# Two lists for the work on the cached keys and the norms, and other steps for each

## The chip, the cores and the metric

The kernel runs on one core of one Trainium2 chip. The metric is the device time of one execution in microseconds. The kernel before was run three times: 2337.23, 2340.57 and 2343.8 us, median 2340.57 us.

## What is computed

One layer of a streaming encoder. A prompt of 2048 rows and a sample of 8 x 16 rows (8 running streams) pass through an adaptive norm and one input projection. Two kinds of attention stand beside each other:

- branch A, differential attention: 4 heads, two score matrices per head, `w = p[0] - lam * p[1]` with `p` a softmax over a chunk-causal mask, then `w @ v`;
- branch B, stick-breaking attention: 8 heads of 64, `log_a = log_sigmoid(z) + cumsum(log_sigmoid(-z), reverse) - log_sigmoid(-z)`, then `exp(log_a) @ v`.

For the 8 streams of the sample the keys and values of 512 earlier positions (`cache_a_k`, `cache_a_v`, `cache_b_k`, `cache_b_v`) stand in front of the new ones. Both branches are gated, multiplied by a branch weight, added, multiplied by `w_out`, added to the input and normed. The outputs are the rows and the new keys and values of both branches.

## The kernel before, in words

**Precision.** Each float32 operand of a large product is scaled by a power of two and split into two float16 halves, `hi` and `lo` (`split`, lines 295 to 304: one instruction for `hi` on ACT, POOL or DVE, one on DVE for `lo`); three products of halves stand for one product. The scale comes from a sum of squares over the whole operand, which has to be there before the first split.

**Units and steps.** After a first stage (the modulated rows `hT_d`, about 135 us) the attention runs in 8 units, `u = 0..7`. An even unit is of kind A (one head of A), an odd unit of kind B (two heads of B). The text calls them A0, B0, A1, B1, A2, B2, A3, B3 or unit 0 to 7. Each unit has 17 steps: `t = NT` (the sample's projection) and `t = 0..15`, one row tile of 128 each. The scores of step t cover t+1 tiles of keys, so the first steps ("small tiles") are short and the last ones long. All is issued by one loop over `steps` (from line 1290); on each engine the instructions run in the order in which the tile scheduler has put them.

In a step run side by side, merged by costs (`interleave`):

- pieces of the projection of a later step (`project`, line 436 ff.: 24 matmuls at L438, in B units also 24 gate matmuls at L514). They run about five steps ahead (`LEAD`);
- the scores of this step (`scores`; matmuls at L649, L650 and the mask's at L653). In A they leave PSUM by a DVE instruction with a running maximum (L568), two exponentials on ACT, a combination and a split on DVE and ACT. In B they leave it by two sigmoids on ACT (L123), a scan on DVE (L626), a product on POOL (L632) and a split;
- the weights of both kinds are then turned by a transposing DMA issued from SP (`wt`, L590);
- the product with the values of the step two before (`pv`, `PV_LAG`; L706 to L708 in A, L710 and L711 in B), which reads `wt`.

All DMAs of these stages are issued by one queue, SP's, in its order.

**The weights of the next unit** (`prepare_unit`, list `back`) are loaded, squared and split during the first steps of a unit. Their buffers, 16 of 4 KB per partition (`wa0..7`, `wb0..7`), come from the list `free`: taken from its front and put back at its end.

**The spare work** is 82 pieces in one list (`norms`, lines 840 to 889):

- 48 *norms* (`one`, L847 for the load): 16 pieces of the output weights and 32 of the cached values. Each takes a buffer from `free`, puts it back at once, loads 512 KB into it and sums its squares with one ACT instruction of 1024 columns (L281);
- 34 pieces for the *cached keys* (`stages`), a pipeline of three stages over 32 blocks of 512 KB: `fetch` (a load, L855), one piece later `square` (one ACT instruction, L281), one piece later `halve`: two small float32 matmuls (L220), four small DVE instructions (L867 to L870), a split with `hi` on POOL (L301) and `lo` on DVE (L304), and a store of 512 KB to `keys_d` (L875). Up to three buffers are held across pieces.

`spare_at` says in which steps pieces of this list are issued; at each such step as many as spread the rest evenly. Before the change it holds at steps 7 to 15 of unit 0, at all 16 steps of units 2, 4 and 6, and at steps 0 to 7 of units 1, 3 and 5: 81 steps for 82 pieces. Taken in order, the norms lie in units 0 to 3 and in steps 0 to 5 of unit 4; the keys lie in steps 6 to 15 of unit 4 (10 pieces), steps 0 to 7 of unit 5 (8) and steps 0 to 15 of unit 6 (16).

Unit 7 has no spare work; there the branch weights are split (`branch_weight`), which waits for the list to be empty. After the units comes a last stage (from about 1840 us): the sample's attention over the cache, the branch products, the output product and the final norm. It reads `keys_d`, the sums of squares and the keys' exponents.

Of the kernel before, what the change touches and what calls it, by code (L numbers as in the profile page):

```python
# [32 lines left out]
NT = SEQ // P  # L33
# [80 lines left out]
def layer_kernel(ctx: ExitStack, tc: tile.TileContext, a: dict):  # L114
# [102 lines left out]
    def total(col, n=1, tag="t"):  # L217

        p = bank(tag)
        T.matmul(p[:, 0:n], ones, col, start=True, stop=True)  # L220
        return p[:, 0:n]
# [54 lines left out]
    def sum_squares(src, n, dst, width=1024, scale=1.0):  # L276

        for i in range(0, n, width):
            junk = tiny.tile([P, width], F16, tag="junk", name="junk", bufs=1)
            w = min(width, n - i)  # L280
            S.activation(out=junk[:, 0:w], in_=src[:, i : i + w], func=AF.Square, scale=scale,  # L281
                         accum_out=dst[:, i // width : i // width + 1])
# [13 lines left out]
    def split(hi, lo, src, s, on=None):  # L296

        if on is S:
            S.activation(out=hi, in_=src, func=AF.Identity, scale=s)  # L299
        elif on is G:  # L300
            G.tensor_scalar(out=hi, in0=src, scalar1=s, scalar2=0.0, op0=ALU.mult, op1=ALU.add)  # L301
        else:
            V.tensor_scalar(out=hi, in0=src, scalar1=s, scalar2=None, op0=ALU.mult)
        V.scalar_tensor_tensor(out=lo, in0=src, scalar=s, in1=hi, op0=ALU.mult, op1=ALU.subtract)  # L304
# [408 lines left out]
    def pv(job):  # L713

        U, t, c = job["U"], job["t"], job["c"]
        segs = job["segs"] if U["kind"] == 0 else job["segs"][::-1]
        order = [(seg, j) for seg in segs for j in range(seg["hi"] - seg["lo"])]

        def block(i):
            seg, j = order[i]  # L720
            if i == 0 and (U["kind"] == 0 or c == 0):
                U["po", t] = bank("o")
            pv_block(job, seg, U["po", t], j, U["v"][seg["lo"] + j], i == 0, i == len(order) - 1)
            if i == len(order) - 1 and (U["kind"] == 0 or c == 1):
                store(U, t, natural(U, t, U.pop(("po", t))))

        return [(1.5, lambda i=i: block(i)) for i in range(len(order))]

    def cache_column(name, h):
        return "ab".index(name[0]) * 4 + h  # L730
# [106 lines left out]
    def norms():  # L837

        srcs = [w[:, k, :] for w in (w_ba, w_bb) for k in range(4)] + [w_out[:, k, :] for k in range(KT)]
        srcs = [(src, wsums[:, i : i + 1], g8 if i < 4 else 1.0) for i, src in enumerate(srcs)]  # L840
        srcs += [(caches[name][:, i * 8 : i * 8 + 8, h * P : (h + 1) * P], csums[:, cache_column(name, h), i : i + 1], 1.0)
                 for name in ("av", "bv") for h in range(4) for i in range(4)]

        def one(src, dst, scale):
            st = free.pop(0)
            free.append(st)
            load(out=st if len(src.shape) == 2 else st.rearrange("p (j n) -> p j n", n=P), in_=src)  # L847
            sum_squares(st, 1024, dst, scale=scale)

        fetched, squared = [], []  # L850

        def fetch(name, h, i):
            st = free.pop(0)
            src = caches[name][:, i * 8 : i * 8 + 8, h * P : (h + 1) * P]
            load(out=st.rearrange("p (j n) -> p j n", n=P), in_=src)  # L855
            fetched.append((st, name, h, i))

        def square():
            acc = tiny.tile([P, 1], F32, tag="cacc", name="cacc", bufs=2)
            sum_squares(fetched[0][0], 1024, acc)  # L860
            squared.append((*fetched.pop(0), acc))

        def halve():
            st, name, h, i, acc = squared.pop(0)
            c = tiny.tile([P, 3], I32, tag="csc", name="csc", bufs=2)
            f = cexp[:, cache_column(name, h), i : i + 1]
            V.tensor_scalar(out=c[:, 0:1].bitcast(F32), in0=total(acc, 1, "s"), scalar1=2.0 ** -46, scalar2=None, op0=ALU.max)  # L867
            V.tensor_scalar(out=f, in0=c[:, 0:1], scalar1=24, scalar2=None, op0=ALU.logical_shift_right)
            V.tensor_scalar(out=c[:, 1:2], in0=f, scalar1=-1.0, scalar2=204.0, op0=ALU.mult, op1=ALU.add)
            V.tensor_scalar(out=c[:, 2:3], in0=c[:, 1:2], scalar1=23, scalar2=None, op0=ALU.logical_shift_left)  # L870
            to = free.pop(0)
            w = P // 2
            x = to.bitcast(F16).rearrange("p (j f n) -> p j f n", f=2, n=w)
            split(x[:, :, 0, :], x[:, :, 1, :], st.rearrange("p (j n) -> p j n", n=w), c[:, 2:3].bitcast(F32), G)
            load(out=keys_d[name, h, i], in_=x.rearrange("p (j c) f d -> p j (c f d)", c=1))  # L875
            free.append(st)
            free.append(to)

        todo = [(name, h, i) for name in ("ak", "bk") for h in range(4) for i in range(4)]

        def stages(k):
            if k > 1:
                halve()
            if 0 < k <= len(todo):
                square()
            if k < len(todo):
                fetch(*todo[k])

        return [lambda x=x: one(*x) for x in srcs] + [lambda k=k: stages(k) for k in range(len(todo) + 2)]

    steps = [(u, t) for u in range(8) for t in [NT] + list(range(NT))]
    back = []
    spare = norms()
    jobs = []


    line = []
# [30 lines left out]
    at = [0]  # L928

    def position(x):  # L930

        m = min(int(x), len(steps) - 1)
        return starts[m] + (starts[m + 1] - starts[m]) * (x - m)
# [8 lines left out]
        at[0] = i  # L942
        return out

    def spare_at(u, t):
        return u < 7 and t < NT and (t >= 7 if u == 0 else u % 2 == 0 or t < 8)

    def duration(t):
        return SAMPLE_TIME if t == NT else TILE_TIME + (t + 1) / 4
# [241 lines left out]
    branch_weights = list(range(8))  # L1191
# [65 lines left out]
    def branch_weight():  # L1257

        i = branch_weights.pop(0)
        if i == 0:  # L1260
            L["wsq"] = con.tile([P, 1], F32, name="wsq")
            V.tensor_copy(out=L["wsq"], in_=total(add_up(wsums[:, 0:8], 8)))
            L["s"] = [scales(L["wsq"], con, "s_w0"), scales(total(add_up(wsums[:, 8:16], 8)), con, "s_w8")]
            L["sa"] = con.tile([P, 1], F32, name="sa")
            V.tensor_tensor(out=L["sa"], in0=L["s"][0][:, 0:1], in1=g8, op=ALU.mult)
            L["wb"] = []
        br, k, j = i // 4, i // 2 % 2 * 2, i % 2
        st, dst = free.pop(0), free.pop(0)
        L["wb"].append(cut(dst.bitcast(F16), st, (w_ba, w_bb)[br], k, j, (L["sa"], L["s"][0][:, 0:1])[br], i // 2))
        free.append(st)  # L1270
# [18 lines left out]
    for n in range(len(steps) + PV_LAG):  # L1289
        made, qk, vs = [], [], []  # L1290
        if n < len(steps):
            u, t = steps[n]
            past += duration(t)
            if t == (3 if u == 0 else NT) and u < 7:
                back += prepare_unit(u + 1)
            if u == 7 and not back and not spare and len(branch_weights) > 1:
                branch_weight()
            for fn in back[: -(-len(back) // max(1, (W_READY if u else W_READY + 2) - t % NT))]:
                back.pop(0)()
            if spare and spare_at(u, t):  # L1300
                left = sum(spare_at(*step) for step in steps[n:])
                for _ in spare[: -(-len(spare) // left)]:
                    spare.pop(0)()
            if t < NT:
                qk = scores(units[u], t, made)
        if n >= PV_LAG:
            for job in jobs[n - PV_LAG]:
                vs += pv(job)
        target = position(len(steps) * past / whole + LEAD)
        pieces = take(target, min(n + 1, len(steps) - 1))  # L1310
        if at[0] == len(line) and not pieces and not spare:
            if cuts is None:
                cuts = early_work()
            pieces = [(1.0, fn) for fn in cuts[: -(-len(cuts) // (len(steps) + PV_LAG - n))]]
            del cuts[: len(pieces)]
        interleave(pieces, qk, (vs, V_LO, V_HI))
        jobs.append(made)
# [158 lines left out]
```

## Time and profile before

| | |
|---|---|
| median of three runs | 2340.57 us |
| the profiled execution: its time, its span | 2343.11 us, 2341.3 us |
| PE busy | 2102.5 us (90%) |
| DVE busy | 1745.7 us (75%) |
| ACT busy | 1624.2 us (69%) |
| POOL busy | 702.6 us (30%) |
| mean granted PE clock | 0.967 |
| share of the 16 DMA engines taken by SP's queue | 75.5% |

The rows shown below come from one execution. A row of the view by stretches of time has, in this order: the stretch (from and to, us from the span's start), its length, then for PE, PEld (weight loads, which run beside matmuls), DVE, ACT and POOL the busy time with the count of instructions in brackets, the granted PE clock, the mean busy share of the DMA engines and what they moved in GB/s. A row of the view of waits names who waited, `<-`, for whom, then the total in us, how often, and the longest. A row of the view by line or tile has minimum, median and maximum in ns, then the first and the last start in us. Stretches are cut where the first score matmul (L649) of a step starts.

### The profile page before, as it was taken

The numbers are of one execution on the slowest core, as the hardware profiler recorded it, in microseconds if no ns is written. First come the engines' busy times: TensorE is split into PE (matmuls) and PEld (weight loads), VectorE is DVE, ScalarE is ACT, GpSimd is POOL, SyncE is SP. The second block draws the span as 40 slices with busy tenths as digits, with TensorE's granted clock in tenths as the row PEclk, the third lists the DMA queues.
The fourth block names the chain that finished last, engine by engine and source line by source line (L and its number), as shares of the span: only waits on it lengthen the run. The fifth ranks groups of instructions, "written<-read, shape, count | busy, mean of one in ns | idle before, by whom it ended". The sixth has DMA issues, their size and how long they took to land. (4 is left out here: it accounts for less than half of the span.)

```text
span 2341.3 us, 41804 instructions
## 1 busy us (share of the span) xinstructions
PE 2102.5 (90%) x14752; PEld 1128.2 (48%) x14752; DVE 1745.7 (75%) x3795; ACT 1624.2 (69%) x3228; POOL 702.6 (30%) x610
## 2 busy tenths in 40 slices
PE   5998899988999898898989988889998689899998
PEld 3654454545555454444544544445454344444443
DVE  4658766779776777977777798887778878677663
ACT  4868677777877777786676786766578666556541
POOL 1223012356400244641033366311335312122111
PEclk8999999999999999999999999999999799999999
DMA  9768667799886778977777789966577899788421
GB/s 335 267 212 222 137 144 174 158 211 198 217 200 146 176 158 202 199 183 183 206 192 185 168 192 229 250 167 165 147 162 168 182 271 260 210 223 215 145 96 55
DMA packets 805827, 445.30 MB, mean 190 GB/s; under 512 B 537354, under 2 KB 744506, under 8 KB 805104
## 3 DMA queue, kind: packets, MB, share of 16 engines
q1 hardware_dynamic: 804668, 442.24, 75.5%
q8 instruction: 115, 1.88, 0.3%
q14 instruction: 96, 0.79, 0.1%
q10 hardware_dynamic: 948, 0.39, 0.1%
HBM read 228.82 MB, written 86.02 MB: 134 GB/s over the span
## 5 line engine op out<-in xcount | busy, mean ns | idle before, releaser
L632 POOL TENSOR_TENSOR sc_p<-sc_p,sc_n 128x127 f32<-128x127 f32 (+7 forms) x192 | 311.3, 1625 | 673.8 <-DVE sc_n L626 650.8
L438 PE MATMUL ps_mm<-wb,hs 128*128 128x512 f16 x1530 | 399.3, 383 | 6.6 <-DMA hs<-hT_d 3.8
L438 PE MATMUL ps_mm<-wa,hs 128*128 128x512 f16 x1590 | 404.3, 380 | 0.8 <-DVE v L304 0.5
L438 PEld LDWEIGHTS <-hs 128*128 128x128 f16 x3120 | 275.6, 99 | 257.0 <-issue 7.8
L626 DVE TENSOR_TENSOR_SCAN sc_n<-ps_s,sc_n,zero_t 128x512 f32<-128x512 f32 x192 | 245.4, 1278 | 72.9 <-ACT ps_s L123 69.2
L649 PE MATMUL ps_s<-k,qst 128*128 128x512 f16 (+3 forms) x640 | 226.7, 355 | 47.2 <-DVE sc_n L626 28.8
L583 DVE TENSOR_TENSOR sc_n<-sc_p,sc_n 128x128 f16<-128x128 f32 (+7 forms) x192 | 213.0, 1115 | 48.2 <-ACT sc_n L582 47.9
L514 PEld LDWEIGHTS <-hs 128*128 128x128 f16 x1632 | 157.1, 99 | 186.9 <-issue 9.6
L514 PE MATMUL ps_t<-wb,hs 128*128 128x512 f16 x1020 | 244.5, 382 | 1.5 <-DVE qst L542 1.5
L123 ACT ACTIVATE sc_p<-ps_s,usc 128x512 f32<-128x512 f32 (+3 forms) x320 | 204.2, 638 | 47.8 <-PE ps_s L650 36.3
L650 PE MATMUL ps_s<-k,qst 128*128 128x512 f16 (+3 forms) x640 | 226.3, 355 | 0.0
L710 PE MATMUL ps_o<-v,wt 128*128 128x128 f16 x1088 | 174.3, 226 | 56.7 <-DMA wt<-sc_n 56.7
L582 ACT CAST sc_n<-sc_p 128x128 f16<-128x128 f32 (+7 forms) x192 | 155.4, 814 | 69.4 <-POOL sc_p L632 69.2
L123 ACT ACTIVATE ps_s<-ps_s,usc 128x512 f32<-128x512 f32 (+3 forms) x328 | 199.2, 607 | 0.0
L1391 PE MATMUL ps_o<-wo,wa 128*128 128x512 f16 x816 | 185.1, 382 | 6.0 <-ACT wo L299 5.3
L710 PEld LDWEIGHTS <-wt 128*128 128x128 f16 x1088 | 106.4, 102 | 122.5 <-DMA wt<-sc_n 68.9
L514 PE MATMUL ps_t<-wa,hs 128*128 128x512 f16 x612 | 157.3, 389 | 6.0 <-ACT qst L542 6.0
L711 PE MATMUL ps_o<-v,wt 128*128 128x64 f16 x1088 | 160.9, 199 | 0.0
L1362 PE MATMUL ps_mm<-wa,wb 128*128 128x512 f16 x510 | 144.2, 390 | 7.8 <-DVE wa L1364 3.4
L568 DVE TENSOR_SCALAR_CACHE_REDUCE sc_p<-ps_s,usc 128x512 f32<-128x512 f32 (+3 forms) x160 | 106.2, 664 | 35.3 <-PE ps_s L650 19.5
L626 DVE TENSOR_TENSOR_SCAN sc_n<-ps_s,zero_t 128x128 f32<-128x128 f32 (+3 forms) x128 | 104.1, 815 | 37.3 <-ACT ps_s L123 36.6
L711 PEld LDWEIGHTS <-wt 128*128 128x128 f16 x1088 | 104.3, 101 | 54.9 <-issue 0.8
(374 smaller groups left out, 4460.3 us busy)
## 6 DMA issues: line engine op xcount, KB each, us to landing
hs<-hT_d SPq DMA_DIRECT2D x130, 512.0 KB, 4.4
g_d<-gt SPq DMA_DIRECT2D x68, 256.0 KB, 4.8
out_dram<-pr SPq DMA_DIRECT2D x204, 64.0 KB, 2.2
wa<-in_w_in_dram SPq DMA_DIRECT2D x40, 256.0 KB, 6.0
o_d<-o SPq DMA_DIRECT2D x136, 64.0 KB, 2.5
wb<-g_d SPq DMA_DIRECT2D x17, 512.0 KB, 3.8
wa<-g_d SPq DMA_DIRECT2D x17, 512.0 KB, 3.4
hs<-o_d SPq DMA_DIRECT2D x17, 512.0 KB, 3.8
```

The source lines that it names most:

```text
L123: i = S.activation(**kw)
L438: T.matmul(box["p"], box["h"][:, hi, k, :], U["w"][k][:, wi, :], start=(n == 0), stop=(n == 3 * KT - 1))
L514: T.matmul(box["g"][:, 0:gw], box["h"][:, hi, k, :], U["wg"][k // per][:, k % per, wi, :], start=(j == 0), stop=(j == 3 * KT - 1))
L582: S.copy(out=hi, in_=src)
L583: V.tensor_tensor(out=lo, in0=src, in1=hi, op=ALU.subtract)
L626: V.tensor_tensor_scan(out=dst[:, lo : lo + n][:, ::-1], data0=src[:, 0:n][:, ::-1], data1=zero_t[:, 0:1].to_broadcast([P, n]), initial=fi ...
L632: G.tensor_tensor(out=p[:, 0:m], in0=p[:, 0:m], in1=n[:, 1 : m + 1], op=ALU.mult)
L649: T.matmul(p[:, 0:n], qst[:, c, :], kk[:, c, 0:n], start=True, stop=False)
L650: T.matmul(p[:, 0:n], qst[:, 2 + c, :], kk[:, c, 0:n], start=False, stop=not diag)
L710: T.matmul(po[:, c * P : (c + 1) * P], wt[:, wj, :], vt[:, c, :, :], start=first, stop=False)
L711: T.matmul(po[:, c * P : c * P + 64], wt[:, nb + wj, :], vt[:, c, 0, :], start=False, stop=last)
L1391: T.matmul(po, st["y"][:, yi * 8 + k, :], wo[j * 4 + k // 2][:, wi, k % 2, :], start=(n == 0), stop=(n == 3 * KT - 1))
```

## The change

`norms` returns two lists instead of one, the 48 norms and the 34 pieces for the keys, and each has its own rule for the steps at which it is issued:

- norms: steps 7 to 15 of unit 0, steps 9 to 15 of units 1 to 5, all steps of unit 6. That is 60 steps for 48 pieces, one at a time, so they end at step 3 of unit 6: 9 in unit 0, 7 each in units 1 to 5, 4 in unit 6;
- keys: steps 0 to 7 of units 1, 3 and 5 and steps 9 to 12 of units 2, 4 and 6. That is 36 steps for 34 pieces: 8, 4, 8, 4, 8 in units 1 to 5 and 2 (steps 9 and 10) in unit 6.

In a step that has both, the norm is issued ahead of the keys' piece. The two tests for an empty list now ask for both. No instruction is added or removed.

```diff
-        return [lambda x=x: one(*x) for x in srcs] + [lambda k=k: stages(k) for k in range(len(todo) + 2)]
+        return [lambda x=x: one(*x) for x in srcs], [lambda k=k: stages(k) for k in range(len(todo) + 2)]
...
-    spare = norms()
+    spare, cached = norms()
...
-    def spare_at(u, t):
-        return u < 7 and t < NT and (t >= 7 if u == 0 else u % 2 == 0 or t < 8)
+    def norm_at(u, t):
+        return u < 7 and t < NT and (t >= 7 if u == 0 else t >= 9 or u == 6)
+
+    def keys_at(u, t):
+        return u in (1, 3, 5) and t < 8 or u in (2, 4, 6) and 9 <= t < 13
...
-            if u == 7 and not back and not spare and len(branch_weights) > 1:
+            if u == 7 and not back and not spare and not cached and len(branch_weights) > 1:
...
-            if spare and spare_at(u, t):
-                left = sum(spare_at(*step) for step in steps[n:])
-                for _ in spare[: -(-len(spare) // left)]:
-                    spare.pop(0)()
+            for todo, here in ((spare, norm_at), (cached, keys_at)):
+                if todo and here(u, t):
+                    left = sum(here(*step) for step in steps[n:])
+                    for _ in todo[: -(-len(todo) // left)]:
+                        todo.pop(0)()
...
-        if at[0] == len(line) and not pieces and not spare:
+        if at[0] == len(line) and not pieces and not spare and not cached:
```

## The prediction, made before the result was known

> **What bounds the kernel now.** I read the page first, then the view by stretches for each unit, then for parts of units, then the waits inside the stretches that differ.
>
> ```profile
> span 2341.3 us, 41804 instructions
> ...
> PE 2102.5 (90%) x14752; PEld 1128.2 (48%) x14752; DVE 1745.7 (75%) x3795; ACT 1624.2 (69%) x3228; POOL 702.6 (30%) x610
> ```
>
> PE works in 90% of the span, and the change neither adds nor removes an instruction. So PE's own work stays, and only the time can change in which PE does not work or works at half clock. The units in which the moved pieces lie (units 1 to 6, one row each):
>
> ```profile
> 317.90:552.50 234.60, 214.85 (x1525) 114.65 (x1524) 179.66 (x275) 184.66 (x380) 97.09 (x79) 0.99 0.79 175
> 552.50:735.90 183.40, 176.82 (x1250) 97.35 (x1248) 140.15 (x382) 141.77 (x317) 43.34 (x46) 0.99 0.81 198
> 735.90:970.20 234.30, 213.86 (x1524) 114.30 (x1523) 180.49 (x276) 185.01 (x381) 97.61 (x79) 0.99 0.79 176
> 970.20:1170.70 200.50, 185.22 (x1273) 102.84 (x1270) 155.70 (x427) 141.29 (x313) 52.33 (x55) 0.96 0.79 194
> 1170.70:1415.90 245.20, 222.00 (x1559) 118.00 (x1556) 197.04 (x317) 186.12 (x383) 112.67 (x88) 0.98 0.80 185
> 1415.90:1613.40 197.50, 176.04 (x1198) 97.04 (x1197) 162.34 (x447) 131.61 (x298) 59.97 (x60) 0.97 0.83 214
> ```
>
> For each row I call *loss* the length less PE's busy time, plus the length times what the granted clock lacks to 1. Unit 1: 234.6 - 214.85 = 19.8, plus 0.01 x 234.6 = 2.3, makes 22.1 us. Units 2 to 6 likewise: 8.4, 22.8, 23.3, 28.1, 27.4. The sum is 132. Unit 2 is an A with 16 norms and no keys; units 4 and 6 are A's with 10 and 16 key pieces and lose 15 and 19 us more. Units 1 and 3 are B's with 8 norms in steps 0 to 7; unit 5 has 8 key pieces there instead and loses 5 to 6 more. The second term is there because idling costs twice:
>
> ```profile
> 558.60:560.60 2.00, 0.03 (x1) 0.03 (x2) 1.97 (x13) 1.97 (x5) 0.47 (x1) 1.00 0.79 183
> 560.80:564.20 3.40, 3.40 (x28) 2.33 (x25) 3.35 (x16) 2.60 (x9) 2.40 (x4) 0.50 0.96 186
> ```
>
> PE idles for 2.0 us, and then 3.4 us run at clock 0.50. The Trainium skill ("TensorE: Matmul & The Clock Gate", Part 1) says that the gate halves the clock after an idle window of about 3.4 us and opens again after as long a busy one. The length of the half-clock stretch agrees; the 2.0 us of idling seen here is shorter than that window, and the measurement decides. By the page alone most of the second term would be zero and the differences between the units smaller.
>
> Where in the units is it lost? B units, steps 0 to 8 (first three rows: units 1, 3, 5) and 9 to 15:
>
> ```profile
> 317.90:421.20 103.30, 96.21 (x642) 50.73 (x641) 73.44 (x134) 81.10 (x181) 30.66 (x31) 0.97 0.70 164
> 735.90:838.30 102.40, 95.36 (x641) 50.47 (x640) 73.73 (x134) 80.92 (x181) 30.59 (x31) 0.98 0.72 165
> 1170.70:1283.40 112.70, 100.52 (x656) 52.39 (x654) 86.79 (x167) 79.43 (x177) 42.51 (x38) 0.95 0.76 190
> 421.20:552.50 131.30, 118.64 (x885) 63.92 (x884) 106.22 (x141) 103.56 (x200) 66.42 (x49) 1.00 0.86 185
> 838.30:970.20 131.90, 118.50 (x884) 63.82 (x883) 106.76 (x142) 104.09 (x201) 67.02 (x49) 1.00 0.85 184
> 1283.40:1415.90 132.50, 121.48 (x905) 65.61 (x903) 110.25 (x151) 106.69 (x206) 70.16 (x51) 1.00 0.82 180
> ```
>
> Losses ahead: 10.2, 9.1 and 17.8 us; behind: 12.7, 13.4, 11.0. A units (2, 4, 6 in each group of three), steps 0 to 8, 9 to 12, 13 to 15:
>
> ```profile
> 552.50:631.70 79.20, 75.26 (x512) 40.45 (x509) 63.27 (x175) 62.74 (x143) 36.21 (x39) 0.98 0.89 221
> 970.20:1054.10 83.90, 78.43 (x534) 41.66 (x531) 68.00 (x185) 65.20 (x149) 38.80 (x41) 0.98 0.83 194
> 1415.90:1509.80 93.90, 84.50 (x544) 44.85 (x543) 79.81 (x223) 64.94 (x149) 48.48 (x48) 0.98 0.90 245
> 631.70:682.10 50.40, 47.76 (x353) 26.62 (x351) 39.73 (x112) 42.73 (x103) 7.13 (x8) 1.00 0.82 204
> 1054.10:1113.90 59.80, 49.99 (x335) 28.89 (x334) 44.42 (x129) 41.14 (x95) 9.06 (x10) 0.91 0.73 184
> 1509.80:1565.00 55.20, 43.53 (x346) 26.35 (x345) 43.42 (x124) 41.18 (x98) 8.13 (x9) 0.96 0.79 183
> 682.10:735.90 53.80, 53.80 (x392) 30.27 (x391) 37.14 (x96) 36.30 (x73) 0.00 (x0) 1.00 0.68 159
> 1113.90:1170.70 56.80, 56.80 (x410) 32.29 (x409) 43.28 (x114) 34.95 (x69) 4.47 (x4) 0.97 0.79 206
> 1565.00:1613.40 48.40, 48.01 (x312) 25.84 (x311) 39.11 (x103) 25.49 (x53) 3.36 (x3) 0.97 0.73 188
> ```
>
> Losses ahead 5.5, 7.1, 11.3; in steps 9 to 12 2.6, 15.2, 13.9; behind 0, 1.7, 1.8. So keys in A cost most in steps 9 to 12, which is where the change puts all A's keys. In unit 4 that stretch looks so:
>
> ```profile
> PEld L706 <- DMA wt<-sc_n: 10.3, 4, 5.8
> ```
>
> ```profile
> SPq L875 <- DVE k L304: 10.8, 1, 10.8
> ```
>
> ```profile
> 1076.11 0.53 SPq L875 DMA_DIRECT2D keys_ak<-wa  x1
> ...
> 1081.21 0.39 SPq L855 DMA_DIRECT2D wa<-in_cache_a_k_dram  x1
> ...
> 1082.79 3.19 SPq L590 DMA_TRANSPOSE wt<-sc_n  x1
> ```
>
> First row: the matmuls with the values wait for the turned weights `wt`. Second and third: SP stands 10.8 us at the store of a key block, whose split is behind other work on DVE; elsewhere the key's store (L875) and load (L855) are among what SP issues ahead of the next transpose, 6.7 us after the store. SP is one queue, and what stands behind the waiting store is `wt`.
>
> **The change, part by part.** One key block costs:
>
> ```profile
> L867 DVE TENSOR_SCALAR csc<-ps_s x32: 125/150/159, 1043.1 to 1595.6; 128x1 f32<-128x1 f32 x32
> ...
> L301 POOL TENSOR_SCALAR wa<-wb,csc x11: 1118/1118/1545, 1043.9 to 1542.9; 128x1024 f16<-128x1024 f32 x11
> L304 DVE SCALAR_TENSOR_TENSOR wa<-wb,csc,wa x11: 1271/1279/2105, 1046.0 to 1545.8; 128x1024 f16<-128x1024 f32 x11
> ```
>
> ```profile
> L220 PE MATMUL ps_s<-cacc,ones x64: 167/250/352, 1042.8 to 1594.7; 128*128 128x1 f32 x64
> ```
>
> On DVE four small instructions of 0.15 and 1.28 us for the low half, together 1.9 us, on POOL 1.12, on PE two matmuls of 0.25, on ACT a square:
>
> ```profile
> L281 ACT ACTIVATE junk<-wa x69: 1039/1057/1208, 34.7 to 1561.4; 128x1024 f16<-128x1024 f32 x69
> ```
>
> A norm costs the same square, 1.06 us on ACT, and one load on SP. Each key piece has a load and a store on SP. All of it is moved, so I price by the loss of the stretch to which it moves.
>
> 1. *Units 1 and 3, steps 0 to 7: 8 key pieces for 8 norms.* The nearest row is unit 5, with the same pieces at the same steps: 17.8 against 10.2 and 9.1, +7.6 and +8.7. But part of unit 5's loss is another wait:
>
> ```profile
> PEld L438 <- DMA hs<-hT_d: 5.4, 3, 3.2
> ```
>
> There SP had the loads of the next unit's weights ahead of the rows `hs` for the projection. In the changed program's order on SP those loads stand at steps 11 and 12 of the B units, no longer at 7. Without this wait and a half-clock stretch after it (half of 3.4 us, as above) unit 5 would lose 17.8 - 5.4 - 1.7 = 10.7. So the ends are +0.5 and +8.7; I take +5, as the load may do the same at its new place. Two units: +10.
>
> 2. *Unit 5* keeps its keys and loses that place of the weights: 0 to -7, I take -3.
>
> 3. *B units, steps 9 to 15: 7 norms each, none before.* PE waits there for the scans, and these partly for ACT (last steps of unit 3):
>
> ```profile
> PE ps_s L649 <- DVE sc_n L626: 8.8, 9, 2.9
> ...
> DVE sc_n L626 <- ACT ps_s L123: 4.5, 3, 3.8
> ```
>
> If all 21 squares fell on that chain it would be 21 x 1.06 = 22 us, if none, 0. The eight norms of units 1 and 3 lay in the front, where the loss is smallest. In the changed order SP issues the loads of the seven norms together at steps 7 and 8, as soon as buffers are free, so most squares come before the scans set the pace. I take +1 per unit: +3.
>
> 4. *Unit 2: 4 key pieces in steps 9 to 12, beside 4 norms; 9 norms of the other steps go.* Ends: 0 and 15.2 - 2.6 = +12.6. Four keys alone made 15.2 in unit 4 and four of unit 6's 13.9, but there the steps before and after had keys as well and handed lateness on. I take +9.
>
> 5. *Unit 4: 4 key pieces stay in steps 9 to 12, 6 go, the norms go to 9 to 15.* Front 7.1 to unit 2's 5.5: -1.6. Steps 9 to 12 from 15.2 to the 11.6 of point 4: -3.6. Behind: -1.7. Sum -7, ends -16 and +3.
>
> 6. *Unit 6: 2 key pieces for 16, 4 norms in the first steps.* Front to 5.5: -5.8. Steps 9 to 12 with half of unit 2's keys: 2.6 + 4.5 = 7.1, from 13.9: -6.8. Behind: -1.8. Sum -14, ends -19 and -6.
>
> 7. *Unit 0* has 9 norms for 10, unit 7 and the last stage are as before: 0. Every piece ends before unit 7, as before, so what waits there for the empty lists does not start earlier or later. PE's work for the keys, 64 x 0.25 us, moves with them and its sum stays.
>
> One rule speaks against B as the keys' place. The Trainium skill ("SBUF — State Buffer", SBUF: two separate sides) says that DVE and GpSimd share a pair of ports as an exclusive lock for a whole instruction, and in B both are at work, POOL with the products. In unit 5 the trace shows a little of it:
>
> ```profile
> L301 POOL TENSOR_SCALAR wa<-wa,csc x2: 1119/1468/1817, 1212.1 to 1235.8; 128x1024 f16<-128x1024 f32 x2
> L304 DVE SCALAR_TENSOR_TENSOR wb<-wa,csc,wb x1: 1815/1815/1815, 1194.3 to 1194.3; 128x1024 f16<-128x1024 f32 x1
> ```
>
> One POOL split has 1.8 us (median 1.12) and one DVE split 1.8 (median 1.28). That is 0.7 us twice in a front half, on engines off PE's path; 16 more pieces in B at that rate make some 3 us of DVE and POOL, and I add nothing.
>
> Sum: 10 - 3 + 3 + 9 - 7 - 14 = -2 us. The profiled execution had 2343.1 us, 2.5 over the median of 2340.57. Measured against the median I forecast 2339 us: a gain in units 4 and 6 of some 21 us is paid back in units 1, 2, 3.
>
> **The rivals.**
>
> *Spread keys cost little (faster).* The loss of units 4 and 6 comes from keys at every step; with four of them units 2 and 4 lose what unit 2 loses now (8.4), unit 6 too: 0 - 15 - 19 = -34, and B pays the full +16 of unit 5's row: -18, or 2323. For it: unit 4's steps 13 to 15 had three pieces and lost only 1.7. Against: steps 9 to 12 lost as much in unit 4 as in unit 6.
>
> *Norms on B's chain (slower).* The squares stand in ACT's order between the sigmoids for which the scans wait, and each load that lands late holds ACT. At full price +22 in place of +3: -2 + 19 = +17, or 2358. It decides from about 11 squares of the 21 on the chain (+9 over my sum). For it: the wait of the scans for ACT above. Against: only the last three steps of a B lose anything.
>
> *SP in A's steps 9 to 12 (slower).* Unit 4 had two spare issues per step there, a load and a store; units 2 and 4 will have three, with the norm's load in front. If `wt` is late in proportion, 15.2 x 1.5 = 22.8 in units 2 and 4 and 11 in unit 6: +20, +4, -11 in place of +9, -7, -14. That is +25 over my sum, 2364.
>
> *It does nothing.* The scheduler pulls loads forward as buffers come free, so the steps written in the rules are not those of the loads, and the loss only changes places: 2341.
>
> **How the numbers follow.** No change that a measurement of this kernel tells is about 0.3%, 7 us. Chances: my sum 0.45 (its own range 2329 to 2349), spread keys cheap 0.25, norms on the chain 0.17, SP in A 0.08, nothing 0.05. Faster by over 7 us (below 2333.5): nearly all of the first rival, 0.24, and a sixth of my case: 0.32. Slower (above 2347.6): both slow rivals, 0.24, and a quarter of my case: 0.35. Same: 0.33. For 8 in 10 the range has to reach to the first rival, 2323, and with the bounds of the norms and SP to 2362.
>
> **What would show it.** Right: units 4 and 6 lose about 16 and 13 us in the view by stretches, units 1 and 3 about 27, and unit 2's steps 9 to 12 show `wt` waits at L706. Wrong: unit 2's steps 9 to 12 still lose about 3 (spread keys are cheap); the last steps of B lose over 20 with scans waiting for ACT (norms); `wt` waits of over 20 us in units 2 and 4 (SP). A different order of projections around the ends of units, which the scheduler sets anew, could move several us that none of these terms holds.

## The result, and the profile after

The median of six runs is 2330.24 us (2323.69 to 2337.64), against 2338.96 us (2337.08 to 2343.8, six runs) for the kernel before in the same comparison. The ratio is 0.9959, with a 95% interval from 0.9942 to 0.9975: 0.41% faster, 9.6 us (the two medians are 8.7 us apart). The profiled executions are further apart: 2326.12 us after, 2343.11 before, a difference of 17.0 us. The term by term account below is of these 17, of which 9 to 10 are the change and the rest the scatter of single executions.

The page after, first rows (busy time, share of the span and count of each engine):

```profile
span 2324.3 us, 41797 instructions
...
PE 2096.5 (90%) x14752; PEld 1123.2 (48%) x14752; DVE 1745.0 (75%) x3795; ACT 1621.7 (70%) x3228; POOL 704.5 (30%) x610
```

PE has the same 14752 matmuls and is busy for 6 us less; its idle time falls from 2341.3 - 2102.5 = 238.8 to 227.8 us. By the view of stretches, units 1 to 6 after (cut, as before, at the first score matmul of the unit):

```profile
317.60:554.30 236.70, 217.97 (x1538) 116.45 (x1537) 189.82 (x306) 187.17 (x387) 105.78 (x85) 0.99 0.84 194
554.30:744.60 190.30, 178.37 (x1260) 97.77 (x1258) 147.29 (x401) 140.08 (x313) 47.96 (x50) 0.99 0.80 191
744.60:988.80 244.20, 219.38 (x1532) 116.64 (x1531) 191.41 (x315) 188.88 (x389) 111.00 (x88) 0.98 0.86 200
988.80:1173.70 184.90, 176.88 (x1265) 97.14 (x1264) 147.90 (x403) 138.41 (x311) 47.51 (x49) 1.00 0.81 195
1173.70:1424.30 250.60, 222.52 (x1550) 118.02 (x1549) 198.62 (x316) 192.66 (x397) 109.65 (x88) 0.99 0.86 202
1424.30:1606.30 182.00, 173.97 (x1242) 96.75 (x1241) 142.92 (x395) 128.23 (x291) 42.45 (x46) 0.99 0.68 162
```

By the measure of the prediction (length less PE's busy time, plus length times the lack of clock) the six units lose 21.1, 13.8, 29.7, 8.0, 30.6 and 9.8 us; before it was 22.1, 8.4, 22.8, 23.3, 28.1 and 27.4. The sum goes from 132 to 113. The clock in the row is rounded to 0.01, which leaves each of these open by 1.3 us at most. Lengths themselves are not compared: units 1 to 6 have 64 PE instructions more than before (the sum of the six counts, 8377 for 8313) and the last stretch has 66 fewer, because the order differs at the ends of units: by line it is mostly products with the values of A (L706 to L708) and gate matmuls (L514) that fall on the other side of a cut.

What PE waited for in units 1 to 6 is seen in the view of waits (who waited, for whom, total us, times, longest). Before:

```profile
PE ps_o L710 <- DMA wt<-sc_n: 31.7, 18, 4.4
PE ps_o L706 <- DMA wt<-sc_n: 24.2, 14, 5.3
PE ps_s L649 <- DVE sc_n L626: 23.1, 28, 2.9
...
PE ps_mm L438 <- DMA hs<-hT_d: 4.0, 4, 3.0
```

After:

```profile
PE ps_s L649 <- DVE sc_n L626: 31.6, 36, 3.4
PE ps_o L710 <- DMA wt<-sc_n: 19.6, 16, 3.3
PE ps_o L706 <- DMA wt<-sc_n: 16.3, 15, 2.6
...
PE ps_mm L438 <- DMA hs<-hT_d: 9.0, 5, 3.0
```

The waits for the turned weights `wt` (both L710 and L706) fall from 55.9 to 35.9 us; the waits for B's scans rise by 8.5 and those for `hs` by 5. This is where PE's waits differ; the experiments ask what brought it.

### The profile page after: what moved, and what is told of

It is laid out like the page before. It is cut to its first block, busy times and chain, and to the rows that moved or that the text cites. A ratio compares the mean times of both kernels' runs of the same rounds, so it can differ in the third digit from the quotient of the medians.

```text
span 2324.3 us, 41797 instructions
## 1 busy us (share of the span) xinstructions
PE 2096.5 (90%) x14752; PEld 1123.2 (48%) x14752; DVE 1745.0 (75%) x3795; ACT 1621.7 (70%) x3228; POOL 704.5 (30%) x610
## 5 line engine op out<-in xcount | busy, mean ns | idle before, releaser
L438 PE MATMUL ps_mm<-wb,hs 128*128 128x512 f16 x1530 | 394.5, 384 | 7.6 <-DMA hs<-hT_d 6.8
L583 DVE TENSOR_TENSOR sc_n<-sc_p,sc_n 128x128 f16<-128x128 f32 (+7 forms) x192 | 222.7, 1163 | 36.8 <-ACT sc_n L582 36.4
L514 PEld LDWEIGHTS <-hs 128*128 128x128 f16 x1632 | 156.5, 98 | 189.1 <-ACT qst L542 5.9
L123 ACT ACTIVATE sc_p<-ps_s,usc 128x512 f32<-128x512 f32 (+3 forms) x320 | 205.1, 641 | 32.5 <-PE ps_s L650 23.3
L514 PE MATMUL ps_t<-wb,hs 128*128 128x512 f16 x918 | 216.1, 379 | 3.0 <-DVE sam L542 1.4
L710 PE MATMUL ps_o<-v,wt 128*128 128x128 f16 x1088 | 168.9, 225 | 43.1 <-DMA wt<-sc_n 42.7
L123 ACT ACTIVATE ps_s<-ps_s,usc 128x512 f32<-128x512 f32 (+3 forms) x328 | 200.5, 611 | 0.0
L1395 PE MATMUL ps_o<-wo,wb 128*128 128x512 f16 x816 | 185.2, 382 | 6.3 <-ACT wo L299 5.5
L514 PE MATMUL ps_t<-wa,hs 128*128 128x512 f16 x714 | 170.6, 381 | 6.9 <-ACT qst L542 5.7
L710 PEld LDWEIGHTS <-wt 128*128 128x128 f16 x1088 | 105.0, 101 | 104.7 <-DMA wt<-sc_n 54.6
L711 PE MATMUL ps_o<-v,wt 128*128 128x64 f16 x1088 | 154.5, 198 | 0.0
L568 DVE TENSOR_SCALAR_CACHE_REDUCE sc_n<-ps_s,usc 128x512 f32<-128x512 f32 (+3 forms) x160 | 106.2, 664 | 35.2 <-PE ps_s L650 17.2
L1366 PEld LDWEIGHTS <-wb 128*128 128x128 f16 x816 | 79.2, 100 | 105.5 <-issue 23.1
L1395 PEld LDWEIGHTS <-wb 128*128 128x128 f16 x816 | 78.7, 98 | 100.4 <-issue 9.1
```

The source lines that it names most:

```text
L123: i = S.activation(**kw)
L438: T.matmul(box["p"], box["h"][:, hi, k, :], U["w"][k][:, wi, :], start=(n == 0), stop=(n == 3 * KT - 1))
L514: T.matmul(box["g"][:, 0:gw], box["h"][:, hi, k, :], U["wg"][k // per][:, k % per, wi, :], start=(j == 0), stop=(j == 3 * KT - 1))
L583: V.tensor_tensor(out=lo, in0=src, in1=hi, op=ALU.subtract)
L710: T.matmul(po[:, c * P : (c + 1) * P], wt[:, wj, :], vt[:, c, :, :], start=first, stop=False)
L711: T.matmul(po[:, c * P : c * P + 64], wt[:, nb + wj, :], vt[:, c, 0, :], start=False, stop=last)
```

## Experiments

The letters in the expectations stand for theories. D: the keys cost where they are dense, and spreading them over fewer pieces per step makes the gain. N: the norms' leaving the small tiles makes it (N1 and N2 are two forms of this). R: neither place matters, and any edit makes the scheduler put the instructions in another order, which is worth as much by chance. S, later on: the steps at which the pieces are issued decide. Each ratio is to the kernel before, run beside it on the same chip; the interval is 95%. The medians of different comparisons are not held against each other: the kernel before has 2338.96, 2342.68, 2346.34 and 2345.04 us in the four of them.

**Each list alone.** The keys at their new steps, the norms at their old ones:

```diff
     def norm_at(u, t):
-        return u < 7 and t < NT and (t >= 7 if u == 0 else t >= 9 or u == 6)
+        return t < NT and (t >= 7 if u == 0 else u == 2 or u in (1, 3) and t < 8 or u == 4 and t < 6)
```

> Only the keys' list moves (steps 0 to 7 of B units, 9 to 12 of A units); the norms stay at the steps of the kernel before. Theory D (dense keys make an A unit lose; thinly spread keys are cheap): most of the gain is here, 2328 to 2333 us, units 4 and 6 lose under 12 us each. Theory N (the gain is that norms left the small tiles): 2336 to 2342, no gain. Theory R (any new order by the scheduler moves several us): anywhere from 2325 to 2345, without units 4 and 6 being the ones that change.

Measured: 2342.97 us, ratio 0.9997 (0.9983 to 1.0011). Thinning out the keys in units 4 and 6 is worth nothing in the time. D falls: by it the whole gain had to show here. But the units do change. Units 1 to 6 of this kernel:

```profile
317.40:559.20 241.80, 220.74 (x1543) 117.61 (x1542) 188.40 (x306) 191.96 (x397) 107.23 (x86) 0.99 0.87 198
559.20:759.20 200.00, 180.56 (x1254) 97.67 (x1253) 146.40 (x402) 144.06 (x321) 42.80 (x49) 0.97 0.79 196
759.20:1003.20 244.00, 222.36 (x1544) 117.86 (x1543) 192.20 (x315) 194.72 (x401) 110.99 (x88) 0.98 0.89 210
1003.20:1192.80 189.60, 180.17 (x1267) 100.13 (x1266) 145.44 (x402) 133.99 (x303) 46.29 (x48) 0.97 0.71 175
1192.80:1436.10 243.30, 217.40 (x1518) 116.16 (x1519) 199.22 (x315) 180.53 (x372) 111.72 (x86) 0.97 0.81 187
1436.10:1621.30 185.20, 176.63 (x1264) 97.30 (x1263) 147.68 (x395) 128.81 (x292) 44.72 (x49) 1.00 0.69 159
```

They lose 23.5, 25.4, 26.5, 15.1, 33.2 and 8.6 us, in sum 132 as before. Units 4 and 6, which the keys left, lose 27 us less, and units 1, 2, 3 and 5 lose that much more. The loss went with the keys, which R as put above did not expect, and its sum stayed.

The norms at their new steps, the keys at their old ones:

```diff
     def keys_at(u, t):
-        return u in (1, 3, 5) and t < 8 or u in (2, 4, 6) and 9 <= t < 13
+        return t < NT and (u == 4 and t >= 6 or u == 5 and t < 8 or u == 6)
```

> Only the norms' list moves (steps 9 to 15 of units 1 to 5, all of unit 6 as long as there are any); the keys stay at steps 6 to 15 of unit 4, 0 to 7 of unit 5, 0 to 15 of unit 6. Theory D: no gain, or a loss where norms now stand beside dense keys: 2337 to 2348, units 4 and 6 lose 20 us or more each. Theory N: 2328 to 2333. Theory R: anywhere from 2325 to 2345.

Measured: 2325.25 us, ratio 0.9924 (0.9904 to 0.9943), better than both together. So far this speaks for N.

**The keys elsewhere in A.** As after, but A's keys at steps 5 to 8:

```diff
-        return u in (1, 3, 5) and t < 8 or u in (2, 4, 6) and 9 <= t < 13
+        return u in (1, 3, 5) and t < 8 or u in (2, 4, 6) and 5 <= t < 9
```

> The changed kernel with A's four key pieces at steps 5 to 8 in place of 9 to 12. Theory D: the number per unit counts, not the step: 2326 to 2334, units 2, 4 and 6 lose 14 us or less. If the steps were what counts (the front of A has the shorter steps, and there wt has less time to arrive), 2336 or more, with the loss in steps 0 to 8 of units 2 and 4. Theory R: 2322 to 2342.

Measured: 2324.79 us, ratio 0.9918 (0.9898 to 0.9937), 0.4% better than after. Units 2, 4 and 6 lose 12.2, 9.3 and 6.7 us, not far from after (13.8, 8.0 and 9.8). With the norms where the change puts them, the keys' steps in A do move the time, but not by more than what follows.

**The order within a step.** As after, but where a step has a norm and a key piece, the key piece is issued first. No piece changes its step.

```diff
-            for todo, here in ((spare, norm_at), (cached, keys_at)):
+            for todo, here in ((cached, keys_at), (spare, norm_at)):
```

> The changed kernel with the keys' piece issued ahead of the norm in the steps that have both (A, 9 to 12). A change that should mean nothing by theory D or N: 2327 to 2333, within 3 us of the changed kernel. Theory R: up to 10 us away from it in either direction.

Measured: 2333.28 us, ratio 0.9962 (0.9947 to 0.9978). After has 0.9959: no difference.

**The keys taken out.** To measure the disputed cost by itself, 31 of the 32 key blocks are left out (the last stage reads the one block that is left for all, and fixed exponents; that block is issued in unit 1 in both), once with the norms at the old steps and once at the new. Nothing else of the work is left out. The main line of the edit:

```diff
-        todo = [(name, h, i) for name in ("ak", "bk") for h in range(4) for i in range(4)]
+        todo = [("ak", 0, 0)]
```

Norms at the old steps:

> The kernel before with 31 of the 32 key blocks left out (the last stage reads the first block for all, so the sample's results are not the reference's); norms at their old steps. Theory N1 (the norms' place costs by itself): slower than the same kernel with the norms at their new steps by 10 to 18 us. Theory N2 (norms cost only where they stand beside keys or hand them lateness and buffers): within 4 us of it. The loss of units 4 and 6 over unit 2 says that all the key work costs some 30 to 45 us, so 2297 to 2313.

Measured: 2305.39 us, ratio 0.9837 (0.9814 to 0.9860).

Norms at the new steps:

> The changed kernel with 31 of the 32 key blocks left out (the last stage reads the first block for all, so the sample's results are not the reference's); norms at their new steps. Theory N1: 10 to 18 us below its counterpart with the norms at the old steps. Theory N2: within 4 us of it.

Measured: 2297.55 us, ratio 0.9792 (0.9769 to 0.9816).

The keys' work costs 1 - 0.9837 = 1.63% or 38 us at its old place, and 0.9959 - 0.9792 = 1.67% or 39 us at its new one: 1.2 us for each block left out, of which two matmuls of 0.25 us are PE's own. Within these intervals, some 0.3% or 7 us, what the key work costs does not depend on where it is put. That is the same answer as that of the first experiment, from the other side. Moving the norms without the keys gave 0.45%, about as much as the whole change. That is 10.5 us by the ratios and 7.8 by the medians, open by 0.3%, and does not decide between N1 and N2.

**The norms' move in halves.** From the kernel before, with its list cut in two as in the change but the keys at their old steps; first only the norms of units 1 and 3 are moved, from steps 0 to 7 to steps 8 to 15:

```diff
+    def norm_at(u, t):
+        return t < NT and (t >= 7 if u == 0 else u == 2 or u in (1, 3) and t >= 8 or u == 4 and t < 6)
+
+    def keys_at(u, t):
+        return t < NT and (u == 4 and t >= 6 or u == 5 and t < 8 or u == 6)
```

> The kernel before with only the norms of units 1 and 3 moved, from steps 0 to 7 to steps 8 to 15. If the gain of the norms' move (17.8 us) lies in the fronts of the B units, 10 us or more of it is here: 2325 to 2333. If it lies in unit 4, where norms stood ahead of the keys, nothing: 2338 to 2346.

Measured: 2309.98 us, ratio 0.9845 (0.9823 to 0.9868): the fastest of all with the whole work, and faster than both kernels of the case.

Then the norms of units 1 and 3 stay and those of the A units go to steps 9 to 15, to unit 5 and to the first steps of unit 6:

```diff
+    def norm_at(u, t):
+        return t < NT and (t >= 7 if u == 0 else u in (1, 3) and t < 8 or u in (2, 4, 5) and t >= 9 or u == 6)
```

> The kernel before with the norms of units 1 and 3 left at steps 0 to 7, those of units 2 and 4 at steps 9 to 15, and the rest in unit 5 (9 to 15) and at the first steps of unit 6. If the gain lies in the B fronts: 2338 to 2346. If it lies in unit 4: 2325 to 2333, with unit 4 losing 14 us or less in place of 23.3.

Measured: 2324.32 us, ratio 0.9906 (0.9885 to 0.9927). Unit 4 loses 13.6 us, as the second case asked; but the first half, which left the norms of unit 4 where they were, gained more.

The halves gain 1.55% and 0.94%; both moves together, measured above, 0.76%. The halves are not quite the whole (units 1 and 3 have eight norms in the first half, seven in the whole), but costs that belong to pieces and steps would come near to adding up; these do not. And in the profile of the first half units 1 and 3 lose 10 us less, and units 2, 4, 5 and 6, where nothing was moved, 27 us less, 16 of them in unit 4. The view of stretches, units 1 to 6 in one row, before:

```profile
317.90:1613.40 1295.50, 1188.79 (x8313) 644.18 (x8312) 1015.38 (x2120) 970.46 (x2070) 463.01 (x404) 0.98 0.80 189
```

With only the norms of units 1 and 3 moved, units 1 to 6 and unit 4 alone (unit 4 before is a row of the prediction):

```profile
317.60:1582.90 1265.30, 1187.48 (x8375) 645.96 (x8374) 1016.71 (x2129) 976.13 (x2082) 465.78 (x404) 0.99 0.83 196
965.50:1147.60 182.10, 176.64 (x1269) 99.59 (x1268) 147.79 (x419) 138.90 (x311) 45.56 (x52) 0.99 0.84 204
```

Unit 4 has the same norms and keys at the same steps in both. It lost 200.5 - 185.22 + 0.04 x 200.5 = 23.3 us before and loses 182.1 - 176.64 + 0.01 x 182.1 = 7.3 now. The prediction had read the price of the keys out of those 23 us.

**The steps kept, the order changed.** This is the test between S and R. In each step the spare pieces are issued ahead of the pieces that prepare the next unit's weights, instead of behind them. Every piece keeps its step; which of them takes a buffer first, and the order that the scheduler makes of it, are new. From the kernel before:

```diff
-            for fn in back[: -(-len(back) // max(1, (W_READY if u else W_READY + 2) - t % NT))]:
-                back.pop(0)()
             if spare and spare_at(u, t):
                 left = sum(spare_at(*step) for step in steps[n:])
                 for _ in spare[: -(-len(spare) // left)]:
                     spare.pop(0)()
+            for fn in back[: -(-len(back) // max(1, (W_READY if u else W_READY + 2) - t % NT))]:
+                back.pop(0)()
```

> The kernel before with the spare piece of a step issued ahead of the next unit's weight pieces of the same step instead of behind them. No piece changes its step, but the scheduler's order changes in most units. Theory S (the steps of the norms and keys decide): within 4 us of the kernel before, 2336 to 2347. Theory R (the order that the scheduler makes of them decides, and any such change moves it): 8 us or more away, in either direction.

Measured: 2320.61 us, ratio 0.9891 (0.9870 to 0.9911). An edit that moves no piece to another step gains 1.1%, more than twice what the change gains.

The same edit to the changed kernel:

> The changed kernel with norms and keys of a step issued ahead of the weight pieces of the same step. Theory S: 2326 to 2337, as the changed kernel (ratio to the kernel before 0.994 to 0.998). Theory R: a ratio outside of that, anywhere from 0.98 to 1.005.

Measured: 2324.15 us, ratio 0.9909 (0.9891 to 0.9928): 0.5% better than after.

The same edit to the kernel with the norms of units 1 and 3 moved:

> The fast variant (only the norms of units 1 and 3 moved to steps 8 to 15, ratio 0.9845) with spare pieces ahead of weight pieces in each step. Theory S: ratio 0.982 to 0.988. Theory R: most of its gain of 36 us is the luck of one order and is lost: ratio 0.990 or more.

Measured: 2350.07 us, ratio 1.0016 (1.0004 to 1.0027). The gain of 1.55% is gone, and the steps are the same. Last, that kernel again with the norms of units 1 and 3 one step earlier, and its order within a step untouched:

```diff
-        return t < NT and (t >= 7 if u == 0 else u == 2 or u in (1, 3) and t >= 8 or u == 4 and t < 6)
+        return t < NT and (t >= 7 if u == 0 else u == 2 or u in (1, 3) and 7 <= t < 15 or u == 4 and t < 6)
```

> The fast variant with the norms of units 1 and 3 at steps 7 to 14 instead of 8 to 15, one step earlier. Theory S: ratio 0.982 to 0.988. Theory R: 0.990 or more.

Measured: 2336.0 us, ratio 0.9949 (0.9930 to 0.9968). Norms one step earlier cost 1.1%.

For the time, S falls and R stands. With the steps fixed, the order, and with it the choice of buffers, moved the time by -1.1%, -0.5%, 0 and +1.7% (1.0016 / 0.9845). Taken by placement, the ratios are 1 and 0.9891 for the steps of before, mean 0.9946; 0.9959, 0.9962 and 0.9909 for those of the change, mean 0.9943; 0.9845 and 1.0016 for the norms of units 1 and 3 moved, mean 0.9931. Two or three orders each are few, but they show no difference between the placements that would stand out from the scatter within one. Nor is the kernel before a middling draw: of eleven edits of it with the whole work, the change included, nine are faster, one is the same (0.9997) and one slower (1.0016), with a mean of 0.9934. A gain of 0.41% is less than the average of these edits brought.

What the order moves can be read from the waits of PE in units 1 to 6. Norms of units 1 and 3 moved (2307.3 us span):

```profile
PE ps_s L649 <- DVE sc_n L626: 21.1, 29, 1.6
PE ps_o L706 <- DMA wt<-sc_n: 14.2, 9, 3.5
PE ps_o L710 <- DMA wt<-sc_n: 11.8, 8, 3.0
...
PE ps_mm L438 <- DMA hs<-hT_d: 0.6, 1, 0.6
```

The same steps in the other order (2343.6 us span):

```profile
PE ps_o L710 <- DMA wt<-sc_n: 14.9, 16, 2.2
PE ps_o L706 <- DMA wt<-sc_n: 14.9, 16, 2.1
PE ps_s L649 <- DVE sc_n L626: 14.2, 18, 2.8
PE ps_mm L438 <- DMA hs<-hT_d: 13.9, 11, 3.2
```

The steps of before in the other order (2318.7 us span):

```profile
PE ps_o L706 <- DMA wt<-sc_n: 21.9, 16, 4.0
PE ps_s L649 <- DVE sc_n L626: 21.2, 28, 2.0
PE ps_o L710 <- DMA wt<-sc_n: 20.4, 19, 2.4
```

PE's waits for `wt` are 55.9 us before, 42.3 in the other order of the same steps, 26.0 with the norms of units 1 and 3 moved and 29.8 in its other order. So these waits do not rank the kernels: the one with 29.8 is no faster than the kernel before with 55.9. In it the wait for `hs` has come up, to 13.9 from 0.6, and PE's busy time, with the same 14752 matmuls, is longer. The stretches say how much, the part ahead of unit 1, units 1 to 6, and the rest. Norms of units 1 and 3 moved:

```profile
0.00:317.60 317.60, 270.09 (x1855) 158.46 (x1856) 202.36 (x607) 219.80 (x461) 51.00 (x74) 0.94 0.76 221
317.60:1582.90 1265.30, 1187.48 (x8375) 645.96 (x8374) 1016.71 (x2129) 976.13 (x2082) 465.78 (x404) 0.99 0.83 196
1582.90:2307.30 724.40, 639.24 (x4525) 322.28 (x4523) 525.42 (x1061) 427.90 (x685) 188.22 (x132) 0.95 0.69 175
```

And the same steps in the other order:

```profile
0.00:320.40 320.40, 271.85 (x1855) 158.26 (x1856) 201.71 (x607) 220.02 (x461) 50.15 (x74) 0.94 0.75 219
320.40:1609.60 1289.20, 1200.29 (x8386) 648.28 (x8385) 1012.22 (x2129) 975.87 (x2081) 470.71 (x404) 0.98 0.82 192
1609.60:2343.60 734.00, 640.69 (x4515) 321.58 (x4515) 521.01 (x1061) 428.44 (x686) 188.82 (x132) 0.94 0.69 173
```

Of the 36.3 us between the spans, 16.0 are PE busy for longer (2112.83 for 2096.81 in sum, at clocks that are 0.01 lower in the second and third rows), and 20.3 are idle. Most of it, 23.9 us, lies in units 1 to 6, and 9.6 in the rest, where neither kernel has a spare piece to move.

Why is `wt` late? The transfers are not seen to be slower. The view of the transposing DMA's line has its time from issue to landing, as its last row, for units 1 to 6, before:

```profile
L590 SPq DMA_TRANSPOSE wt<-sc_n x216: 1167/1812/5918, 320.8 to 1610.7; - x108
...
DMA to landing us min/median/max: 2.3/4.4/7.3
```

and with the norms of units 1 and 3 moved:

```profile
L590 SPq DMA_TRANSPOSE wt<-sc_n x216: 1172/1826/6087, 320.5 to 1571.2; - x108
...
DMA to landing us min/median/max: 2.4/4.5/6.9
```

The median is 4.4 and 4.5 us, while PE's waits for it halve. That speaks for the moment of issue as what differs, but does not prove it: the trace tells the landing of only 26 of the 216 transposes before and 24 here, and PE may also come later to its products. One such moment was quoted in the prediction: SP standing 10.8 us at a key's store in unit 4. In the kernel with the norms of units 1 and 3 moved SP's longest stand at a key's store in units 1 to 6 is 3.1 us (the second and third row, its two largest groups; the third number is the longest):

```profile
SPq L590 <- DVE sc_n L304: 32.8, 8, 11.2
...
SPq L875 <- DVE wa L304: 8.7, 7, 3.1
...
SPq L875 <- DVE wb L304: 5.7, 4, 2.6
```

With the keys at the same steps, the longest stand at a key's store is 10.8 us in one order and 3.1 in another. A long stand of SP is not by itself a loss, though: in the faster kernel SP stands up to 11.2 us at a transpose whose data is not ready (first row). Which reordering, on which engine, makes `wt` late was not isolated. Nor was a kernel tried that keeps the order of all engines but one, or changes the order and keeps the buffers.

## Why the prediction was right, and where it was not

The forecast was 2339 us with a range of 2323 to 2362, and 2329 to 2349 for the case of its own. The measured 2330.24 lies in both, near the faster end. The outcome, faster by over 0.3%, had a chance of 0.32. That the time lies in the range says little for the working: an order alone moved the time by up to 1.1% down and 1.7% up, and either would have put it outside. That this order did not was luck.

Point by point, as losses of the profiled executions in us:

| term | forecast | measured |
|---|---|---|
| 1. units 1 and 3, steps 0 to 8 | +10 | +0.4 and +8.8 |
| 2. unit 5, steps 0 to 8 | -3 | -2.2 |
| 3. B units, steps 9 to 15 | +3 | -1.1, -0.9 and +5.0 |
| 4. unit 2 | +9 | +5.4 |
| 5. unit 4 | -7 | -15.3 |
| 6. unit 6 | -14 | -17.6 |
| sum | -2 | -17.5 |

A minus is a smaller loss. The sum of the measured column lies near the 17.0 us between the profiled executions. Terms 1 to 3 come from these rows, the B units after, steps 0 to 8 (units 1, 3, 5) and then 9 to 15:

```profile
317.60:423.80 106.20, 97.72 (x660) 52.28 (x659) 80.56 (x162) 80.22 (x178) 37.85 (x37) 0.98 0.80 202
744.60:857.10 112.50, 100.22 (x658) 52.83 (x657) 85.80 (x171) 80.18 (x177) 42.92 (x38) 0.95 0.82 209
1173.70:1288.70 115.00, 102.87 (x664) 53.57 (x663) 81.47 (x168) 81.32 (x180) 41.57 (x38) 0.97 0.80 207
423.80:554.30 130.50, 120.25 (x880) 64.17 (x879) 109.26 (x144) 106.95 (x209) 67.93 (x49) 0.99 0.88 187
857.10:988.80 131.70, 119.16 (x876) 63.81 (x875) 105.61 (x145) 108.70 (x212) 68.08 (x50) 1.00 0.88 192
1288.70:1424.30 135.60, 119.64 (x888) 64.45 (x887) 117.15 (x148) 111.34 (x218) 68.08 (x50) 1.00 0.92 198
```

Losses ahead: 10.6, 17.9, 15.6; behind: 11.6, 12.5, 16.0. Terms 1, 2 and 3 were right as sums. The +9 of term 1 came from unit 3 alone, with unit 1 at +0.4, though both got the same eight key pieces at the same steps: one execution does not give a price per piece. Term 2 was right in size and wrong in its cause. The loads of the weights did leave step 7 of unit 5, but the wait for `hs` in its front, which was to go with them, rose from 5.4 to 7.6 us; what fell is the wait for `wt`, from 9.7 to 5.3:

```profile
PEld L438 <- DMA hs<-hT_d: 7.6, 3, 3.1
...
PEld L710 <- DMA wt<-sc_n: 5.3, 4, 2.7
```

Terms 4 to 6 took 11.6 us for steps 9 to 12 of an A with four keys and 7.1 for unit 6 with two. These steps after, units 2, 4 and 6:

```profile
629.40:686.30 56.90, 52.08 (x357) 28.39 (x356) 45.36 (x127) 43.53 (x102) 12.22 (x13) 0.97 1.01 245
1065.30:1117.80 52.50, 49.38 (x356) 27.34 (x356) 43.10 (x122) 41.95 (x99) 11.43 (x13) 1.00 1.05 254
1505.10:1549.80 44.70, 41.14 (x282) 22.95 (x280) 38.84 (x107) 31.00 (x75) 3.66 (x4) 0.96 0.65 155
```

They lose 6.5, 3.1 and 5.4 us. Here the step that failed is the reading "keys in A cost most in steps 9 to 12". It was read from units 4 and 6 of before, where those steps lost 15.2 and 13.9. Units 2 and 4 now have four keys and four norms there, a norm more in each step than unit 4 had, and lose 6.5 and 3.1. The other three kernels with the keys at these steps lose 3.8 to 8.9 there. And the 15.2 was one order's figure: the seven kernels that keep the keys at the steps of before lose between 3 and 16 us in these steps of unit 4.

As sizes, then, terms 4, 5 and 6 were off by 4, 8 and 4 us, all to the slow side, and the rest close. Of the prediction's own signs, units 4 and 6 were to lose about 16 and 13 us and lose 8.0 and 9.8, units 1 and 3 about 27 and lose 21.1 and 29.7. A small reading is off too: the long DVE split in the front of unit 5 is 0.5 us over its median, not 0.7; no term rests on it.

How much of this is the place of the pieces, and how much one order? Twelve profiled kernels have the whole work. Seven keep the keys at the steps of before, five have them moved. The mean loss of each unit in the five less that in the seven, in us, beside the forecast of the terms put together by unit:

| unit | forecast | keys moved less keys kept |
|---|---|---|
| 1 | +6 | +4.2 |
| 2 | +9 | +7.1 |
| 3 | +6 | +8.6 |
| 4 | -7 | -2.6 |
| 5 | -2 | -1.1 |
| 6 | -14 | -13.7 |
| sum | -2 | +2.5 |

Each kernel counts with one execution, and in most of the five the norms were moved too. In two units the place of the keys stands out from the orders: unit 6 loses 15.3 to 31.0 us with its sixteen key pieces and 6.7 to 10.3 with two, unit 3 loses 26.5 to 31.5 with eight and 18.7 to 25.4 without. Unit 4 does not show it: with the same ten key pieces it loses anything from 7.3 to 23.3. So the loss of a stretch has both in it, the pieces and the order. The idea under the terms, that what units 4 and 6 gain is paid back in units 1, 2 and 3, is borne out by these means and by the keys moved alone, 0.9997; so is a sum near zero. What failed is that each price was read from one execution of one order, and that the order had no term. Of the 17.5 us that this pair gains the forecast had 2; the other orders do not show the rest to be the price of keys or norms.

The waits for `wt` at L706 and L710, on which the prediction built, are what moved most in this pair, from 55.9 to 35.9 us. Over all orders they do not decide the time, as the kernel with 29.8 us of them and 1.0016 shows.

The rivals. *Spread keys cost little* forecast 2323 and the losses of units 4 and 6 (8.0 and 9.8) as they came, but 8.4 for unit 2, which loses 13.8; and with the keys moved alone what units 4 and 6 saved was lost in the others. *Norms on B's chain*: the scans' waits did rise from 23.1 to 31.6 us, 8.5 of the 19 that the rival asked for, but not the time; and the kernel with the norms of units 1 and 3 on that chain has 21.1. *SP in A's steps 9 to 12* is excluded by the 6.5 and 3.1 above. *It does nothing*, with a chance of 0.05, said that the steps in the rules are not those of the loads and the loss only changes places. As a mechanism this and the prediction's own sum were nearest to what the runs show, though the one new order that was drawn came out 9.6 us ahead. The last sentence of the prediction, that an order set anew could move several us that no term holds, named it and gave it no price. Measured, its size is between 1.1% down and 1.7% up, some 25 to 40 us, which is more than every term of the sum.

So the 0.41% is a real difference between two programs, and it is not shown to be a property of the placement.

## What to carry to other kernels

Where a list scheduler sets the order of all engines, price an edit only together with a control that changes the order and nothing else; if such controls scatter by a per cent, a gain of 0.4% says nothing of the idea behind the edit. The loss of a stretch in one profile says where time is lost, and not yet what the pieces in it cost, as unit 4 went from 23.3 to 7.3 us when pieces of other units were moved: compare several orders, take the work out, or move one list alone, before putting a price on its place. And add up all the stretches: here the loss followed the keys from unit to unit and its sum stayed. And if a null reordering gains 1.1%, trying several orders is itself a way to tune: one order with the norms of units 1 and 3 in steps 8 to 15 has 0.9845, the best time found here with the whole work.

## What was not expected of the hardware

Two things. The transposing DMA took a median of 4.4 and 4.5 us from issue to landing, where the trace tells it, in the kernels that waited for it 55.9 us and 26.0 us, at 189 and 196 GB/s on 0.80 and 0.83 of the DMA engines: a heavier load on them did not go with a later `wt`. And programs differ in how far their own runs spread: after 2323.69 to 2337.64 us (six runs), the keys at steps 5 to 8 2321.6 to 2325.66 (six runs), the last experiment 2324.64 to 2340.27 (eight). A single execution can thus stand 7.4 us (after) or 11.4 us (the last) from its program's median, as much as the change, which is why the 17 us between the two profiled executions had to be held against the 8.7 between the medians.
